# Chunks of the output weights asked for earlier and in program order, and the second half's low parts on VectorE

## The chip, the core and the metric

The kernel runs on one core of a Trainium2 chip. The metric is the device time of one launch in microseconds. A core has TensorE (PE, matmuls), VectorE (DVE), ScalarE (ACT), GpSimd (POOL) and SyncE (SP, which issues the DMAs here), each with its own queue of instructions. An engine takes its queue in order, and instructions on different engines wait for each other by semaphores.

## The reference

One layer of a hybrid block on 1024 tokens (and 16 meta tokens ahead of them) of width 1024, in f32. Cut to the part that matters:

```
z = einsum('bld,dn->bln', rmsnorm(h), w_in)      # pooled part, attention, gates ga and gb
...
o = rmsnorm(o, gla_norm) * silu(r)               # chunked gated linear attention
y_b = einsum('blc,cd->bld', o, w_gla_out)        # 512 -> 1024
m = sigmoid(ga) * y_a + sigmoid(gb) * y_b        # the merge
h = h + einsum('bld,de->ble', m, w_out)          # the out projection, 1024 -> 1024
h = h + squared_relu_mlp(rmsnorm(h, norm_ffn))
```

## The kernel before, in words

Every f32 matmul is made of three matmuls on split operands: a number is stored as a high part (rounded to the type fp32r) and a low part (what is left), and `mm3` (L246 to L248) adds high by high, high by low and low by high in PSUM. So an operand costs two steps before TensorE can use it: ACT copies it into the high part, and DVE or GpSimd subtracts that from it for the low part.

The stretch at stake lies between the end of the attention and the out projection, and runs once. It has two parts.

The blocks. `yb_block(n, h)` computes y_b and the merge for one half h of the sequence (512 tokens) and 256 of the 1024 columns, in two units. A unit is 12 matmuls into one PSUM bank, then on DVE L1093 (times the gate gb) and L1094 (plus the gated y_a, loaded from memory), then on ACT L1097, the high part `th`, and on GpSimd L1098, the low part `tl`. The gates `gl` and `ml` come from memory into `t` and `o` buffers by `yb_load` (L1041, L1042), a few units ahead. Half 0 runs while the attention's second half closes (L1299 to L1314 are the attention's last norm and its result `yg`, which half 1 needs); half 1 has four blocks, eight units, called units 1 to 8 below. Each block needs a weight of w_gla_out, split by `W1`: loaded to a raw buffer (L101), high part L77 on ACT, low part L78 on DVE or GpSimd. Half 1 uses two weights that half 0 left in place, then two new ones, whose splits follow units 2 by 2.

The out projection. `out_tile(t, ch)` makes 128 tokens by 512 columns with 24 matmuls, from `th`/`tl` of all columns and `wo`, the split of w_out. The half `ch` of w_out comes in four chunks of 256 rows: `load_wo(ch, kk)` loads a chunk to a raw buffer (L101), ACT makes the high part (L1378), DVE the low part (L1379). Matmuls 1 to 6 of a tile read chunk 0, 7 to 12 chunk 1, and so on. Then DVE adds the bank to `acc` (L1411), into which `x_again` (L1370) has loaded x.

`acc` is 32 KB of each partition and lies over what the attention used until its end, among it the buffers `t1` and `o` of half 0's units.

What sets the order. Steps are called in one order of the program, and a scheduler places the instructions of each engine by when it expects them to be ready. From `early_gates` to `wo1_open` that is switched off for ACT and DVE: their queues hold the steps in the order of the program. SP's queue is placed by the scheduler. The steps of half 1 and of the out projection are:

```
yb(0), yb(1), load_wo(0,0), yb(2), load_wo(0,1), yb(3), load_wo(0,2), load_wo(0,3), wo1_open,
x_again(0), out_tile(0,0), x_again(1), out_tile(1,0), x_again(2), out_tile(2,0), load_wo(1,0), ...
```

Of the kernel before, what the change touches and what calls it, by code (L numbers as in the profile page):

```python
# [58 lines left out]
class Ring:  # L59


    def __init__(self, nc, raw, hi, lo, depth):
        self.nc, self.raw, self.hi, self.lo, self.depth = nc, raw, hi, lo, depth
        self.queue, self.loaded, self.done, self.kept = [], 0, 0, 0
        self.views = {}
        self.eng = nc.vector

    def top_up(self):
        while self.loaded < min(self.done + self.depth, len(self.queue)):
            ap = self.queue[self.loaded]  # L70
            s = self.loaded % self.depth
            n = 1
            for k in ap.shape[1:]:
                n *= k
            raw = self.raw.load(ap, n)
            hi, lo = self.hi[:, s, :n], self.lo[:, s, :n]
            self.nc.scalar.activation(hi, raw, ACT.Copy)  # L77
# [28 lines left out]
def kernel(  # L106
# [934 lines left out]
        nc.sync.dma_start(gl, gb_dram[d, h])  # L1041
        nc.sync.dma_start(ml, ma_dram[d, h])  # L1042

    def in_order(on):


        if on:
            S["order"] = tc.manual_schedule(engines={mybir.EngineType.Activation, mybir.EngineType.DVE})
            S["order"].__enter__()
        else:  # L1050
            S.pop("order").__exit__(None, None, None)
# [14 lines left out]
    def yb_block(n, h):  # L1066
        j = YB[h][n]

        def fn(*wbs):
            if h == 0 and n > 1:  # L1070
                kept[j] = wbs[0]
            wb = wbs[0] if wbs else kept[j]
            hi, lo = (t.rearrange("p (k c) -> p k c", k=4) for t in wb)
            assert h or ("o", 0) in done
            yg = S["yg"][h]
            for e in range(2):
                d, w = 2 * j + e, slice(e * P, (e + 1) * P)
                for m in range(2 + h):
                    yb_load(2 * n + e + m, h)
                gl, ml = staged[2 * n + e, h]  # L1080
                b = bank("mm")
                for k in range(4):
                    mm3(
                        b, 1, lambda i: (hi[:, k, w], lo[:, k, w]),
                        lambda i: (yg[:, 0, k], yg[:, 1, k]), first=k == 0, last=k == 3,
                    )
                    yield 3 * 512 / 2400
                if e and not wbs:
                    W1.done, W1.kept = W1.done + 1, W1.kept - 1
# [3 lines left out]
                dve.tensor_tensor(gl, b, gl, ALU.mult)  # L1093
                dve.tensor_tensor(gl, gl, ml, ALU.add)  # L1094
                th = MH[h][:, d]
                tl = ML[h][:, d]
                act.activation(th, gl, ACT.Copy)  # L1097
                pool.tensor_tensor(tl, gl, f32(th), ALU.subtract)  # L1098

        return fn  # L1100

# [256 lines left out]
    def merge_open():  # L1358
# [4 lines left out]
        S["wo"] = [left.push("wo0", [P, 2, KT, HALF], F32R)]  # L1363
        S["left_acc"] = left.mark()
        S["acc"] = left.push("acc", [P, 8, D], F32)
        raw.lend(S["raw3"])
        nc.sync.dma_start(gB, bcast(norm_ffn))

    def x_again(t):
        nc.sync.dma_start(S["acc"][:, t], x[t * P : (t + 1) * P, :])  # L1370

    def load_wo(ch, kk):
        def fn():
            wo = S["wo"][ch][:, :, 2 * kk : 2 * kk + 2]
            c = slice(ch * HALF, (ch + 1) * HALF)
            r = raw.load(w_out[kk * 256 : (kk + 1) * 256, c].rearrange("(k p) c -> p k c", p=P), D)
            r = r.rearrange("p (k c) -> p k c", k=2)
            act.activation(wo[:, 0], r, ACT.Copy)  # L1378
            dve.tensor_tensor(wo[:, 1], r, f32(wo[:, 0]), ALU.subtract)  # L1379

        return fn

    step(one, merge_open)
    def wo1_open():
        in_order(False)
        raw.back()
        right.pop_to(0)
        buffer("u2", 2, D)
# [343 lines left out]
```

## Time and profile before

| what | value |
|---|---|
| median of 3 runs | 1234.57 us (1233.56 to 1236.65) |
| the profiled execution | 1233.45 us, span 1231.7 us |
| TensorE busy in the span | 1204.4 us, 98% |
| DVE, ACT, GpSimd busy | 851.8, 618.7 and 64.4 us |
| matmuls | 6818 |
| data moved | 173.84 MB |

The profile is of one execution. Its rows name a line of the kernel, an engine, an operation and the buffers as out<-in; "b_..." are PSUM banks. A time in brackets is the idle time of the engine just before the instruction, with what ended it. Matmuls overlap, so the row of one shows 0.39 us where one starts every 0.23 us.

### The profile page before, as it was taken

What the parts mean: (1) busy time and instruction counts of PE and PEld (TensorE: products, weight loads), DVE (VectorE), ACT (ScalarE), POOL (GpSimd) and SP (SyncE); (2) the same over time, 40 slices, a digit from 0 to 9 for tenths busy, and PEclk for the clock granted to TensorE, in tenths of its full rate; (3) what the DMA queues carried; (4) which work ended last, traced back from release to release, by engine and by line L of the source; (5) the groups of instructions that cost most, each with busy time, mean ns of one, the idle gap of its engine ahead of it and who ended that gap; (6) DMA issues with size and microseconds to landing.
All of it is one profiled execution on the core that took longest, in us unless ns stands there. A gap on an engine that the chain in (4) does not pass through costs nothing.

```text
span 1231.7 us, 18293 instructions
## 1 busy us (share of the span) xinstructions
PE 1204.4 (98%) x6818; PEld 1003.1 (81%) x6818; DVE 851.8 (69%) x1391; ACT 618.7 (50%) x1099; POOL 64.4 (5%) x70
## 2 busy tenths in 40 slices
PE   7999999999999999899999999999999999999997
PEld 7878888978887888688878888888888888888886
DVE  7986675753566676624896676776765887887686
ACT  7667567322446753312654454554554444444554
POOL 2000000001101115300000000000000000000000
PEclk9999999999999999899999999999999999999999
DMA  8043426155112156831244444444469973333532
GB/s 252 2 112 118 121 86 188 52 171 188 36 36 71 60 156 213 294 99 52 99 125 160 156 154 139 163 154 143 163 222 314 345 264 95 98 99 95 164 99 87
DMA packets 141672, 173.84 MB, mean 141 GB/s; under 512 B 9944, under 2 KB 81392, under 8 KB 141584
## 3 DMA queue, kind: packets, MB, share of 16 engines
q1 hardware_dynamic: 141552, 172.62, 43.8%
q8 instruction: 53, 0.87, 0.3%
q14 instruction: 35, 0.29, 0.1%
q0 software_dynamic: 32, 0.07, 0.1%
HBM read 119.17 MB, written 53.48 MB: 140 GB/s over the span
## 4 chain that ended last, share of the span: by engine, by line
PE 85%; DVE 9%; ACT 3%; issue 2%; DMA 1%; POOL 0%; SPq 0%; DVEq 0%; ACTq 0%; POOLq 0%
PE b_mm L246 10%; PE b_mm L247 10%; PE b_mm L248 10%; PE b_ms L247 9%; PE b_ms L246 9%; PE b_ms L248 9%; PE b_x L247 8%; PE b_x L248 8%; PE b_x L246 8%; PE b_sc L1180 1%; PE b_mx L246 1%; PE b_m L1282 1%; PE b_mx L247 1%; PE b_mx L248 1%; DVE t L1093 1%
## 5 line engine op out<-in xcount | busy, mean ns | idle before, releaser
L246 PE MATMUL b_mm<-th,w1h 128*128 128x512 f32 (+1 forms) x312 | 117.6, 377 | 1.4 <-DVE c L794 1.0
L247 PE MATMUL b_mm<-tl,w1h 128*128 128x512 f32 (+1 forms) x312 | 116.0, 372 | 0.6 <-DVE tl L1440 0.6
L248 PE MATMUL b_mm<-th,w1l 128*128 128x512 f32 (+1 forms) x312 | 115.8, 371 | 0.0
L246 PE MATMUL b_x<-th,w1h 128*128 128x512 f32 (+1 forms) x240 | 90.7, 378 | 0.0
L247 PE MATMUL b_x<-tl,w1h 128*128 128x512 f32 (+1 forms) x240 | 90.6, 378 | 0.0
L248 PE MATMUL b_x<-th,w1l 128*128 128x512 f32 (+1 forms) x240 | 90.3, 376 | 0.0
L264 ACT ACTIVATE w1h<-raw 128x512 fp32r<-128x512 f32 x96 | 59.5, 621 | 34.2 <-PE b_x L247 14.2
L265 DVE TENSOR_TENSOR w1l<-raw,w1h 128x512 fp32r<-128x512 f32 x96 | 65.6, 684 | 10.5 <-ACT w1h L264 10.5
L246 PEld LDWEIGHTS b_mm<-th,w1h 128*128 128x128 f32 x312 | 58.6, 188 | 13.1 <-issue 1.4
L264 ACT ACTIVATE w1h<-fs 128x512 fp32r<-128x512 f32 x72 | 45.4, 631 | 45.8 <-PE b_ms L247 31.3
L247 PEld LDWEIGHTS b_mm<-tl,w1h 128*128 128x128 f32 x312 | 58.6, 188 | 10.6 <-DVE tl L1440 0.9
L248 PEld LDWEIGHTS b_mm<-th,w1l 128*128 128x128 f32 x312 | 58.6, 188 | 10.3
L264 ACT ACTIVATE w1h<-bt 128x512 fp32r<-128x512 f32 x44 | 27.8, 632 | 67.9 <-issue 63.6
L265 DVE TENSOR_TENSOR w1l<-fs,w1h 128x512 fp32r<-128x512 f32 x72 | 49.3, 685 | 14.7 <-ACT w1h L264 14.6
L1589 DVE TENSOR_TENSOR bt<-w,w 128x512 f32<-128x512 f32 x80 | 54.6, 683 | 2.1 <-DMA w<-in_w_ff_dram 2.1
L248 PEld LDWEIGHTS b_x<-th,w1l 128*128 128x128 f32 x240 | 45.1, 188 | 8.4
L246 PEld LDWEIGHTS b_x<-th,w1h 128*128 128x128 f32 x240 | 45.0, 188 | 8.5
L247 PEld LDWEIGHTS b_x<-tl,w1h 128*128 128x128 f32 x240 | 45.1, 188 | 8.3
L264 ACT ACTIVATE fxh<-bt 128x512 fp32r<-128x512 f32 x36 | 22.8, 632 | 54.9 <-issue 49.3
L247 PE MATMUL b_ms<-wo,w1h 128*128 128x512 f32 x128 | 49.8, 389 | 0.0
L246 PE MATMUL b_ms<-wo,w1h 128*128 128x512 f32 x128 | 49.8, 389 | 0.0
L248 PE MATMUL b_ms<-wo,w1l 128*128 128x512 f32 x128 | 49.8, 389 | 0.0
(445 smaller groups left out, 3353.9 us busy)
## 6 DMA issues: line engine op xcount, KB each, us to landing
hf_dram<-h SPq DMA_DIRECT2D x112, 256.0 KB, 2.1
raw<-hf_dram SPq DMA_DIRECT2D x112, 256.0 KB, 2.7
w<-in_w_ff_dram SPq DMA_DIRECT2D x64, 256.0 KB, 5.0
raw<-in_w_in_dram SPq DMA_DIRECT2D x24, 512.0 KB, 4.8
raw<-in_w_ff_dram SPq DMA_DIRECT2D x16, 512.0 KB, 4.2
rawx<-in_w_ff_dram SPq DMA_DIRECT2D x16, 512.0 KB, 4.1
xs<-in_x_dram SPq DMA_DIRECT2D x8, 512.0 KB, 5.9
rawx<-in_w_in_dram SPq DMA_DIRECT2D x8, 512.0 KB, 4.3
```

The lines of the kernel that those rows point to most:

```text
L246: pe.matmul(ps, ah, bh, start=first and i == 0, stop=False, skip_group_check=more)
L247: pe.matmul(ps, ah, bl, start=False, stop=False, skip_group_check=more)
L248: pe.matmul(ps, al, bh, start=False, stop=last and i == n - 1, skip_group_check=more)
L264: act.activation(hi, a, ACT.Copy)
L265: dve.tensor_tensor(lo, a, f32(hi), ALU.subtract)
L1093: dve.tensor_tensor(gl, b, gl, ALU.mult)
L1180: pe.matmul(b[to, e, j], kk[r, s], qq[r, s], start=True, stop=True, tile_position=(e * CH, u * CH))
L1282: pe.matmul(o[part(u), e, j], scc[part(u), e, j], v[part(u), j, e], start=j == 0, stop=False, tile_position=(u * CH, u * CH), skip_group_c ...
L1589: dve.tensor_tensor(bt, w, S["w2"][q[3:]][:, i], ALU.add if q[2] == "+" else ALU.subtract)
```

## The change

Lines below `fetch` have numbers 6 to 24 higher after the change: L1093, L1094, L1097 and L1098 become L1100, L1101, L1104 and L1105, L78 becomes L84, L1378 and L1379 become L1402 and L1403, and L1411 becomes L1435. A fetch of w_out into acc or into the buffer `raw3` stands at L1394, the gain of the next norm (`gB`) at L1380, x at L1383.

- A chunk of w_out can be asked for (`fetch_wo`) apart from its split. Chunk 0 is fetched in `early_gates`, into the buffer `raw3`, which was unused until `merge_open` and is no longer lent to the raw buffers. Chunk 1 is fetched in `merge_open`, into the sixth tile of `acc`, chunk 2 behind block 0 into the seventh, and chunk 3 behind block 1 into the eighth. The two new weights of half 1 are asked for in `merge_open` too (`W1.fetch(2)`).
- The splits `load_wo(0, n)` stand ahead of block n of half 1, not behind it.
- From `merge_open` to `first_blocks` SP's queue holds its DMAs in the order of the program.
- In half 1 the low part `tl` is made on DVE.
- The load of gB stands behind the blocks, and x is asked for two tiles ahead.

```diff
+    def fetch(self, count):
+        for ap in self.queue[self.loaded + len(self.fetched) :][:count]:
             ...
+            self.fetched.append((self.raw.load(ap, n), n))
...
     def early_gates():
-        in_order(True)
+        in_order("order", mybir.EngineType.Activation, mybir.EngineType.DVE)
...
         S["raw3"] = right.push("raw3", [P, D], F32)
+        fetch_wo(0, 0, S["raw3"])
         for n in range(3):
             yb_load(n, 1)
...
                 act.activation(th, gl, ACT.Copy)
-                pool.tensor_tensor(tl, gl, f32(th), ALU.subtract)
+                (dve if h else pool).tensor_tensor(tl, gl, f32(th), ALU.subtract)
...
         S["acc"] = left.push("acc", [P, 8, D], F32)
-        raw.lend(S["raw3"])
+        any_order("order")
+        in_order("loads", mybir.EngineType.SP)
+        in_order("order", mybir.EngineType.Activation, mybir.EngineType.DVE)
+        W1.fetch(2)
+        fetch_wo(0, 1, S["acc"][:, 5])
+
+    def load_gB():
         nc.sync.dma_start(gB, bcast(norm_ffn))
...
+    def fetch_wo(ch, kk, at=None):
+        c, rows = slice(ch * HALF, (ch + 1) * HALF), w_out[kk * 256 : (kk + 1) * 256]
+        ap = rows[:, c].rearrange("(k p) c -> p k c", p=P)
+        if at is None:
+            at = raw.load(ap, D)
+        else:
+            nc.sync.dma_start(at.rearrange("p (k c) -> p k c", k=2), ap)
+        fetched[ch, kk] = at.rearrange("p (k c) -> p k c", k=2)
...
     for n, j in enumerate(YB[1]):
+        step(one, load_wo(0, n))
         if n < 2:
             step(one, yb_block(n, 1))
         else:
             step(one, yb_block(n, 1), W1, [rows4(w_gla_out, j)])
-        if n:
-            step(one, load_wo(0, n - 1))
-    step(one, load_wo(0, 3))
+        if n < 2:
+            step(one, lambda kk=n + 2: fetch_wo(0, kk, S["acc"][:, 4 + kk]))
+    step(one, load_gB)
     step(one, wo1_open)
+    step(one, lambda: x_again(0))
+    step(one, lambda: x_again(1))
     for t in range(8):
-        step(one, lambda t=t: x_again(t))
+        if t < 6:
+            step(one, lambda t=t: x_again(t + 2))
         step(one, out_tile(t, 0))
...
     def first_blocks():
+        any_order("loads")
```

TensorE's instructions stand in the same order before and after. On SP, at the attention's close, this stood before (a number behind a buffer's name is its place in memory; t_2709 and o are the gates of half 0, t_4531 and o_4535 those of half 1, mix is the attention's):

```order
L1299 DMA mix<-r_dram 128x2x512
L101 DMA raw_119<-in_w_gla_out_dram 128x4x256
L101 DMA raw_4539<-in_w_gla_out_dram 128x4x256
L1042 DMA o<-ma_dram 128x512
L1041 DMA t_2709<-gb_dram 128x512
L1042 DMA o<-ma_dram 128x512
L1041 DMA t_2709<-gb_dram 128x512
L1042 DMA o<-ma_dram 128x512
L101 DMA raw_115<-in_w_out_dram 128x2x512
L1041 DMA t_2709<-gb_dram 128x512
L1042 DMA o<-ma_dram 128x512
```

And this stands there now, on from the same load of mix:

```order
L1306 DMA mix<-r_dram 128x2x512
L107 DMA raw_119<-in_w_gla_out_dram 128x4x256
L1048 DMA o<-ma_dram 128x512
L1047 DMA t_2709<-gb_dram 128x512
L1048 DMA o<-ma_dram 128x512
L1047 DMA t_2709<-gb_dram 128x512
L107 DMA raw_115<-in_w_gla_out_dram 128x4x256
L1047 DMA t_2709<-gb_dram 128x512
L1048 DMA o<-ma_dram 128x512 x2
L1047 DMA t_2709<-gb_dram 128x512
L1394 DMA acc<-in_w_out_dram 128x2x512
L1047 DMA t_4531<-gb_dram 128x512
```

The second new weight has moved behind four gates of half 0, and chunk 0's load is gone from here (it stands well ahead). Chunk 1's fetch into acc is behind the last gate of half 0, with half 1's gates behind it. Ahead of these rows, around the load of half 0's last weight, SP had:

```order
L1041 DMA t_4531<-gb_dram 128x512 x3
L1042 DMA o_4535<-ma_dram 128x512 x3
L101 DMA raw_115<-in_w_gla_out_dram 128x4x256
L1026 DMA gb_dram<-o 128x512
L1041 DMA t_2709<-gb_dram 128x512 x2
L1042 DMA o<-ma_dram 128x512 x2
```

and now has:

```order
L1047 DMA t_4531<-gb_dram 128x512 x3
L1394 DMA raw_4539<-in_w_out_dram 128x2x512
L1048 DMA o_4535<-ma_dram 128x512 x2
L1032 DMA gb_dram<-o 128x512
L1048 DMA o_4535<-ma_dram 128x512
L1047 DMA t_2709<-gb_dram 128x512 x2
L1048 DMA o<-ma_dram 128x512 x2
L107 DMA raw_115<-in_w_gla_out_dram 128x4x256
```

The weight has moved behind four gates of half 0, and chunk 0's fetch stands among half 1's first gates. On DVE, units 1 to 4 of half 1 read like this before (th and tl are the merged result, tl not made here; raw_4539 is the second new weight):

```order
L1093 TENSOR_TENSOR t_4531<-b_mm,t_4531 128x512
L1094 TENSOR_TENSOR t_4531<-t_4531,o_4535 128x512
L78 TENSOR_TENSOR w1l<-raw_119,w1h 128x1024
L1093 TENSOR_TENSOR t_4531<-b_x,t_4531 128x512
L1094 TENSOR_TENSOR t_4531<-t_4531,o_4535 128x512
L1093 TENSOR_TENSOR t_4531<-b_x,t_4531 128x512
L1094 TENSOR_TENSOR t_4531<-t_4531,o_4535 128x512
L78 TENSOR_TENSOR w1l<-raw_4539,w1h 128x1024
L1093 TENSOR_TENSOR t_4531<-b_mm,t_4531 128x512
L1094 TENSOR_TENSOR t_4531<-t_4531,o_4535 128x512
L1379 TENSOR_TENSOR wo_4804<-raw_115,wo_4804 128x1024
```

and units 1 to 3 read like this now:

```order
L1100 TENSOR_TENSOR t_4531<-b_mm,t_4531 128x512
L1101 TENSOR_TENSOR t_4531<-t_4531,o_4535 128x512
L1105 TENSOR_TENSOR tl_143<-t_4531,th_139 128x512
L84 TENSOR_TENSOR w1l<-raw_119,w1h 128x1024
L1100 TENSOR_TENSOR t_4531<-b_x,t_4531 128x512
L1101 TENSOR_TENSOR t_4531<-t_4531,o_4535 128x512
L1105 TENSOR_TENSOR tl_143<-t_4531,th_139 128x512
L1403 TENSOR_TENSOR wo_4805<-acc,wo_4805 128x1024
L1100 TENSOR_TENSOR t_4531<-b_x,t_4531 128x512
L1101 TENSOR_TENSOR t_4531<-t_4531,o_4535 128x512
L1105 TENSOR_TENSOR tl_143<-t_4531,th_139 128x512
L84 TENSOR_TENSOR w1l<-raw_115,w1h 128x1024
```

Each unit has a third instruction, L1105, and chunk 1's split (from acc) stands behind unit 2, where the first split of a chunk stood behind unit 4. Chunks 2 and 3 follow behind units 4 and 6. Chunk 0's split has moved further up, into the attention's close, where DVE had this:

```order
L1093 TENSOR_TENSOR t_2709<-b_mm,t_2709 128x512
L1094 TENSOR_TENSOR t_2709<-t_2709,o 128x512
L1287 COPY small<-b_m_4639 128x2
L1093 TENSOR_TENSOR t_2709<-b_mm,t_2709 128x512
L1094 TENSOR_TENSOR t_2709<-t_2709,o 128x512
L1304 TENSOR_REDUCE small<-mix 128x8
```

and now has this:

```order
L1100 TENSOR_TENSOR t_2709<-b_mm,t_2709 128x512
L1101 TENSOR_TENSOR t_2709<-t_2709,o 128x512
L1294 COPY small<-b_m_4640 128x2
L1100 TENSOR_TENSOR t_2709<-b_mm,t_2709 128x512
L1403 TENSOR_TENSOR wo_4805<-raw_4539,wo_4805 128x1024
L1101 TENSOR_TENSOR t_2709<-t_2709,o 128x512
L1311 TENSOR_REDUCE small<-mix 128x8
```

The low part of chunk 0 (L1403) stands between the two instructions of one unit of half 0, ahead of the norm's sum (L1304, now L1311).

More of the change, by code (lines that the diff above doesn't have):

```diff
@@ L63, in __init__ @@
         self.nc, self.raw, self.hi, self.lo, self.depth = nc, raw, hi, lo, depth
-        self.queue, self.loaded, self.done, self.kept = [], 0, 0, 0
+        self.queue, self.loaded, self.done, self.kept, self.fetched = [], 0, 0, 0, []
         self.views = {}
         self.eng = nc.vector
[L68 to L71, printed above, removed]
+    def fetch(self, count):
+        for ap in self.queue[self.loaded + len(self.fetched) :][:count]:
             n = 1
@@ L74, in top_up @@
                 n *= k
-            raw = self.raw.load(ap, n)
+            self.fetched.append((self.raw.load(ap, n), n))
+    def top_up(self):
+        while self.loaded < min(self.done + self.depth, len(self.queue)):
+            s = self.loaded % self.depth
+            if not self.fetched:
+                self.fetch(1)
+            raw, n = self.fetched.pop(0)
             hi, lo = self.hi[:, s, :n], self.lo[:, s, :n]
@@ L1042, in yb_load, with in_order, any_order @@
         nc.sync.dma_start(ml, ma_dram[d, h])
[L1044 to L1051, printed above, removed]
+    def in_order(key, *engines):
+        S[key] = tc.manual_schedule(engines=set(engines))
+        S[key].__enter__()
+    def any_order(key):
+        S.pop(key).__exit__(None, None, None)
     def early_gates():
-        in_order(True)
+        in_order("order", mybir.EngineType.Activation, mybir.EngineType.DVE)
         left.pop_to(S["left_n"])
@@ L1370, in x_again @@
         nc.sync.dma_start(S["acc"][:, t], x[t * P : (t + 1) * P, :])
+    fetched = {}
+    def fetch_wo(ch, kk, at=None):
[6 more added lines that the diff above has]
+        fetched[ch, kk] = at.rearrange("p (k c) -> p k c", k=2)
     def load_wo(ch, kk):
         def fn():
[L1374 to L1377, printed above, removed]
+            if (ch, kk) not in fetched:
+                fetch_wo(ch, kk)
+            wo, r = S["wo"][ch][:, :, 2 * kk : 2 * kk + 2], fetched.pop((ch, kk))
             act.activation(wo[:, 0], r, ACT.Copy)
@@ L1384, in wo1_open @@
     def wo1_open():
-        in_order(False)
+        any_order("order")
         raw.back()
```

## The prediction

> **What bounds the kernel now.** I began with the page, then went through windows of 20 us to find where TensorE is not full in the stretch that the change touches, then read that place in TensorE's timeline, in the waits and in windows of 2 us.
>
> ```profile
> span 1231.7 us, 18293 instructions
> 500.00:520.00 20.00, 13.88 (x55) 10.32 (x54) 14.10 (x16) 8.24 (x11) 6.92 (x6) 0.89 0.93 320
> 520.00:540.00 20.00, 20.00 (x85) 16.41 (x84) 9.48 (x12) 5.25 (x7) 0.00 (x0) 0.94 0.63 193
> ```
>
> The columns after the length are the busy time of PE, weight loads, DVE, ACT and GpSimd, then the granted clock, the DMA share and GB/s. TensorE is busy 13.88 of 20 us and then all of it, so it is the bound on both sides of one hole: there, and only there, a microsecond saved is one at the end. TensorE's timeline (start, duration, idle before and its releaser) gives the hole's shape:
>
> ```profile
> 488.35 0.39 PE L247 MATMUL b_mm<-yg,w1h 128*128 128x512 f32 x1
> ...
> 503.53 0.39 PE L248 MATMUL b_x<-yg,w1l 128*128 128x512 f32 x1
> ...
> 505.80 0.39 PE L246 MATMUL b_mm<-yg,w1h 128*128 128x512 f32 x1
> ...
> 508.52 0.39 PE L246 MATMUL b_mm<-wo,th 128*128 128x512 f32 x1
> ...
> 511.83 0.50 PE L247 MATMUL b_mm<-wo,th 128*128 128x512 f32 x1 [1.37 <-DVE wo L1379]
> ...
> 517.31 0.79 PE L246 MATMUL b_mm<-wo,th 128*128 128x512 f32 x1 [4.06 <-ACT wo L1378]
> ...
> 518.80 0.79 PE L247 MATMUL b_mm<-wo,th 128*128 128x512 f32 x1 [0.69 <-DVE wo L1379]
> ...
> 519.82 0.63 PE L246 MATMUL b_mm<-wo,th 128*128 128x512 f32 x1
> ...
> 522.38 0.49 PE L246 MATMUL b_mm<-wo,th 128*128 128x512 f32 x1
> ...
> 523.17 0.39 PE L246 MATMUL b_x<-wo,th 128*128 128x512 f32 x1
> ...
> 534.05 0.39 PE L246 MATMUL b_mm<-wo,th 128*128 128x512 f32 x1
> ```
>
> The first two rows belong to the blocks and are used below. 505.80 is the first matmul of the last unit (12 matmuls) of the second half, 508.52 that of out tile 0 (24), 523.17 that of tile 1, 534.05 that of tile 3. A unit takes 2.72 us, one matmul 2.72 / 12 = 0.227, a tile in steady state (534.05 - 523.17) / 2 = 5.44. Tile 0 takes 14.65: **9.21 us too much**, the ceiling of what the change can return here. Idle makes 1.37 + 4.06 + 0.69 = 6.12 of it, most of the rest is a slower clock (six matmuls from 519.82 to 522.38, 0.43 each). What was waited for (us in total, times, the longest), and windows of 2 us:
>
> ```profile
> DVE wo L1379 <- ACT wo L1378: 7.1, 4, 3.0
> ACT wo L1378 <- DMA raw<-in_w_out_dram: 6.1, 2, 3.1
> PE b_mm L246 <- ACT wo L1378: 4.1, 1, 4.1
> ...
> 512.00:514.00 2.00, 1.25 (x5) 0.69 (x5) 1.17 (x3) 0.63 (x1) 0.16 (x1) 1.00 0.81 279
> 514.00:516.00 2.00, 0.00 (x0) 0.00 (x0) 1.62 (x2) 0.32 (x1) 1.10 (x1) 0.94 0.83 236
> 516.00:518.00 2.00, 0.69 (x1) 0.29 (x1) 0.71 (x1) 2.00 (x3) 1.27 (x1) 0.50 1.03 383
> ```
>
> The chain is: chunk of w_out still in flight, ACT's high part, DVE's low part, TensorE. The loads come late at 236 to 383 GB/s, and after the idle the clock stands at 0.50.
>
> **The change part by part.** TensorE's instructions keep their order. (1) The four chunks are asked for early, so the load ahead of ACT's split goes. (2) Eight low parts of the second half go from GpSimd to DVE, ahead of the chunk's split. (3) Chunk 0's split moves up into the attention's close. What is late next is DVE, whose queue now holds everything. Its prices, and those of its partners ACT and GpSimd, from their timelines and one group of the page:
>
> ```profile
> 473.90 0.69 DVE L1093 TENSOR_TENSOR t<-b_mm,t 128x512 f32<-128x512 f32 x1 [0.74 <-PE b_mm L248]
> 474.63 0.69 DVE L1094 TENSOR_TENSOR t<-t,o 128x512 f32<-128x512 f32 x1
> ...
> 485.97 1.23 DVE L1314 TENSOR_TENSOR yg<-mix,yg 128x1024 fp32r<-128x1024 f32 x1 [1.13 <-ACT yg L1313]
> ...
> 489.78 0.68 DVE L1093 TENSOR_TENSOR t<-b_mm,t 128x512 f32<-128x512 f32 x1
> 490.49 1.07 DVE L1094 TENSOR_TENSOR t<-t,o 128x512 f32<-128x512 f32 x1
> ...
> 504.17 1.47 DVE L1379 TENSOR_TENSOR wo<-raw,wo 128x1024 fp32r<-128x1024 f32 x1 [1.65 <-ACT wo L1378]
> 505.56 0.68 DVE L1093 TENSOR_TENSOR t<-b_mm,t 128x512 f32<-128x512 f32 x1
> ...
> 520.94 1.21 DVE L1379 TENSOR_TENSOR wo<-rawx,wo 128x1024 fp32r<-128x1024 f32 x1
> 473.71 1.06 ACT L77 ACTIVATE w1h<-raw 128x1024 fp32r<-128x1024 f32 x1 [0.39 <-PE b_mm L247]
> 475.35 0.63 ACT L1097 ACTIVATE th<-t 128x512 fp32r<-128x512 f32 x1 [0.58 <-DVE t L1094]
> 502.55 0.63 ACT L1097 ACTIVATE th<-t 128x512 fp32r<-128x512 f32 x1 [3.23 <-DVE t L1094]
> 503.09 1.05 ACT L1378 ACTIVATE wo<-raw 128x1024 fp32r<-128x1024 f32 x1
> 492.68 1.29 POOL L1098 TENSOR_TENSOR tl<-t,th 128x512 fp32r<-128x512 f32 x1
> L265 DVE TENSOR_TENSOR w1l<-raw,w1h 128x512 fp32r<-128x512 f32 x96 | 65.6, 684 | 10.5 <-ACT w1h L264 10.5
> ```
>
> The new operation on DVE has a direct price: L265's low part of the same size takes 0.68 (GpSimd takes 1.29). A unit on DVE, counted from the start of L1093: L1094 0.71 later (489.78 to 490.49), done after 0.69, th 0.03 behind that (474.63 + 0.69 to 475.35), so th starts at 1.43; it takes 0.63, and the low part runs from 2.09 to 2.77. The next L1093 starts at about 2.72: **2.7 a unit**, TensorE's own pace. Where a weight split stands behind the unit, ACT starts its high part 0.54 behind th (502.55 to 503.09), it takes 1.05, DVE's low part starts 0.03 later (504.14 to 504.17), at 3.05, and takes 1.21 to 1.22 with GpSimd quiet; the next L1093 starts 0.08 before its end (504.17 + 1.47 against 505.56): **4.19 a unit**, 1.47 more than TensorE needs. Splits stand behind units 1 and 3 (weights of the blocks) and 2, 4 and 6 (chunks 1, 2, 3).
>
> Start of the line. Chunk 0's low part now sits between L1093 at 473.90 and its L1094, so that L1094, th, the norm behind it and yg come about 1.16 later. From 485.97 on DVE ran without a gap, so unit 1 starts at 489.78 + 1.16 = 490.94. TensorE first reads yg's low part at 488.35 and it was done at 487.20: 1.15 of cover, so TensorE loses at most 0.1 there; without that cover it would lose the whole 1.16. Unit 1 pays 0.38 more, since GpSimd still works at the first half's last low part (L1094 took 1.07 for 0.69): 4.57.
>
> The Trainium skill (SBUF — State Buffer, "Who interferes with whom") says that a DVE instruction with two inputs in SBUF and a GpSimd instruction that reads SBUF lock each other out for a whole instruction. By that rule unit 1 would lose up to a whole GpSimd instruction, 1.29, and the sum would come out 0.9 us later; the rows bear out the contention, but only in part of its size (0.38 here).
>
> Chunk 1. Its fetch goes into acc, which lies over buffers that GpSimd's last first-half low part reads. Before, the first load into acc was let go by the same event, which SP's queue shows (its first two rows are for the rivals):
>
> ```profile
> 461.63 0.38 SPq L101 DMA_DIRECT2D raw<-in_w_gla_out_dram  x1
> ...
> 465.70 1.89 SPq L1042 DMA_DIRECT2D o<-ma_dram  x2
> ...
> 484.89 0.32 SPq L1041 DMA_DIRECT2D t<-gb_dram  x1
> 492.74 0.33 SPq L1370 DMA_DIRECT2D acc<-in_x_dram  x1
> DMA to landing us min/median/max: 3.8/6.5/8.8
> DMA to landing us min/median/max: 3.9/5.7/7.1
> ```
>
> The first landing row is of the loads into acc, the second of those into raw, both for 455 to 545. The fetch is issued at 492.74 + 1.16 = 493.9. I take the shortest landing, 3.8, since nothing was issued since 484.89 and the queues are empty; bounds 3.8 and 8.8. It lands at 497.7, and ACT could take it at 490.94 + 4.57 + 1.43 + 0.54 = 497.48: 0.2 late, so unit 2 takes 4.4. Chunk 2 stands on SP behind the gates that take unit 1's buffers, free at 490.94 + 2.8, so it leaves by 494.4 and ACT wants it behind unit 4's th, at 490.94 + 4.57 + 4.4 + 4.19 + 1.97 = 506.1; chunk 3 stands behind the gates that take unit 3's buffers (499.9 + 2.8) and leaves by 503.6, wanted at 513.0. Both have more than the longest landing, 8.8, and are costed at nothing; were that cover gone, each us would be one at the end.
>
> Sum: 490.94 + 4.57 + 4.4 + 4.19 + 4.19 + 2.72 (unit 5) + 4.27 (unit 6 to the end of chunk 3's low part, 3.05 + 1.22) = 515.28. TensorE, never held, would read that low part at matmul 19 of tile 0 and one more, 508.52 + 18 x 0.227 + 0.23 = 512.83. So TensorE is **2.45 late** in place of 9.21. Of these, 0.65 appear earlier, at the weights behind unit 3: 490.94 + 4.57 + 4.4 + 4.27 = 504.18 against the read at 503.53. With some 0.2 for restarts 2.65, and the gain is 9.21 - 2.65 = about 6.5. The out tiles need x and the norm gain behind the chunks on SP: x for tile 0 comes late for DVE, but its bank is wanted again only four tiles on, over 10 us of cover. Unit 8's low part stands behind that too and is read by tile 4, near 533.
>
> The profiled execution spans 1231.7 and lasts 1233.45; the median of the runs is 1234.57, 1.1 above. The sum gives 1226.95 for the former and **1228.1** for the latter.
>
> **The rivals.** *Chunk 1 lands late* (0.18): at acc's median of 6.5 it stands at 500.4, 2.9 late, and the gain is 6.5 - 2.7 = 3.8, 1230.8; at 8.8 it is 5.2 late, the gain 1.5, 1233.1. For it speak the 320 GB/s of that stretch before, against it the queues that are empty when the fetch leaves.
>
> *The clock drops once more* (0.08). Two short stalls remain, 0.65 and about 1.8. A stall of 1.37 kept 1.00, one of 4.06 brought 0.50. If the two trip it all the same, nine matmuls at 0.43 instead of 0.23 cost 1.8: 1229.9, still faster. The Trainium skill (TensorE: Matmul & The Clock Gate, "Part 1: The HAM clock gate (the "warmup" mystery)") says that the clock halves after an idle window of about 3.4 us; by that it would stay full here, and the trace agrees, with full clock behind 1.37 and half behind 4.06.
>
> *Slower* (0.12): SP's program order holds the load of the first half's last weight block, issued at 461.63 before, behind four more gate loads, the last two of which left at 465.70 to 467.59; it leaves at about 468. ACT's high part of it (473.71 before) stands ahead of a th (475.35 before, 476.5 with chunk 0's split) and of the norm's first step. It takes 1.06, so the point from which it decides is a landing at 475.5: each us behind that moves the norm, yg and DVE's whole line by one. The gain of 6.5 is used up at 482; at 486 it is 4.0 slower, 1238.6. Against it: raw's longest landing, 7.1, gives 475.1. For it: the load would have to wait for one more transfer ahead of it, and no row shows that queue with its loads held in program order, so more waits there are possible.
>
> That the change does not do what it says is excluded by the order of the instructions, in which SP's fetches and DVE's low parts stand where it puts them.
>
> **How the numbers follow.** 0.3%, 3.7 us, is what a measurement of this kernel can tell from no change. The forecast has 0.62; its own range runs from the ceiling (gain 9.2, 1225.4) to a chunk 1 that lands 2.7 later (1230.8). With the clock rival, faster has 0.70. The late landing lies mostly within the bound, 0.18, and slower has 0.12. The range goes from 1225.4 to 1233.1, the end of the late landing, and leaves out the slower case.
>
> **What would show it.** Right: out tile 0 takes some 8 us in place of 14.65; the longest stall in it is under 2.5 and its releaser DVE's low part of chunk 3; no wait of ACT for w_out over 1 us; the clock near 1.00; yg 1.1 to 1.2 later than before. Wrong: ACT waiting for acc's DMA for several us; ACT's high part of the gla weights waiting for DMA near 475 with TensorE idle behind it.

## The result and the profile after

The changed kernel takes 1231.51 us (median of 12 runs, 1227.94 to 1233.01) against 1234.16 for the kernel before (12 runs): a ratio of 0.9978, interval 0.9970 to 0.9985. It is faster, by 2.65 us where 6.5 were forecast. Run again later on one chip beside the kernel before, it took 1230.16 against 1234.24, ratio 0.9969 (0.9958 to 0.9980).

The profiled execution took 1232.42 us, its span is 1230.7. Windows of 20 us, with the columns as before:

```profile
480.00:500.00 20.00, 18.45 (x85) 14.78 (x84) 16.37 (x24) 6.32 (x10) 6.59 (x5) 1.00 0.36 113
500.00:520.00 20.00, 17.68 (x75) 13.46 (x74) 14.37 (x19) 7.07 (x9) 0.00 (x0) 1.00 0.64 207
520.00:540.00 20.00, 20.00 (x90) 16.59 (x89) 9.75 (x12) 4.88 (x5) 0.00 (x0) 1.00 0.90 335
```

From 500 to 520 TensorE is busy 17.68 us in place of 13.88, at full clock. But it now idles from 480 to 500 too, where it was full; this is that row of the kernel before:

```profile
480.00:500.00 20.00, 20.00 (x94) 16.65 (x93) 15.24 (x19) 7.49 (x10) 10.57 (x7) 1.00 0.45 143
```

TensorE's timeline after:

```profile
483.70 1.09 PE L1317 MATMUL b_m<-ident,mix 128*128 128x128 f32 x8 [1.53 <-DVE mix L1313]
...
505.41 0.50 PE L252 MATMUL b_x<-yg,w1h 128*128 128x512 f32 x1 [0.54 <-ACT w1h L83]
...
506.67 0.50 PE L254 MATMUL b_x<-yg,w1l 128*128 128x512 f32 x1 [0.52 <-DVE w1l L84]
...
511.80 0.39 PE L252 MATMUL b_mm<-wo,th 128*128 128x512 f32 x1
...
516.53 0.50 PE L252 MATMUL b_mm<-wo,th 128*128 128x512 f32 x1 [0.49 <-ACT wo L1402]
...
517.79 0.50 PE L253 MATMUL b_mm<-wo,th 128*128 128x512 f32 x1 [0.76 <-DVE wo L1403]
...
519.06 0.39 PE L252 MATMUL b_x<-wo,th 128*128 128x512 f32 x1
...
620.75 0.49 PE L252 MATMUL b_mm<-th,w1h 128*128 128x512 f32 x1 [0.89 <-ACT th L1463]
...
621.88 0.50 PE L253 MATMUL b_mm<-tl,w1h 128*128 128x512 f32 x1 [0.64 <-DVE tl L1464]
```

Out tile 0 runs from 511.80 to 519.06, 7.26 us in place of 14.65, and its stalls are short. It starts 3.28 later than before, though (508.52), because TensorE idled 1.53 us ahead of the norm's transposes (L1317) and 0.54 and 0.52 in the blocks, and lost some more at each restart. Tile 1 starts at 519.06 against 523.17, 4.11 earlier. The execution was already 0.44 us ahead at the start of the stretch (L1093 at 473.90 before, L1100 at 473.46 now), so the change brought 4.11 - 0.44 = **3.67 us** here. This lead at out tile 1, less what stood at the start, is the measure used below.

DVE's line, then the rows of GpSimd, ACT and SP that explain it:

```profile
473.46 0.69 DVE L1100 TENSOR_TENSOR t<-b_mm,t 128x512 f32<-128x512 f32 x1 [0.73 <-PE b_mm L254]
474.07 1.22 DVE L1403 TENSOR_TENSOR wo<-raw,wo 128x1024 fp32r<-128x1024 f32 x1
475.20 2.90 DVE L1101 TENSOR_TENSOR t<-t,o 128x512 f32<-128x512 f32 x1
479.71 1.22 DVE L1311 TENSOR_REDUCE small<-mix 128x8 f32<-128x1024 f32 x1 [1.61 <-ACT mix L1308]
...
492.36 0.68 DVE L1100 TENSOR_TENSOR t<-b_mm,t 128x512 f32<-128x512 f32 x1
...
496.94 0.68 DVE L1100 TENSOR_TENSOR t<-b_x,t 128x512 f32<-128x512 f32 x1
...
502.34 0.68 DVE L1100 TENSOR_TENSOR t<-b_x,t 128x512 f32<-128x512 f32 x1
...
506.54 0.68 DVE L1100 TENSOR_TENSOR t<-b_mm,t 128x512 f32<-128x512 f32 x1
...
513.46 0.69 DVE L1100 TENSOR_TENSOR t<-b_x,t 128x512 f32<-128x512 f32 x1
...
516.51 1.23 DVE L1403 TENSOR_TENSOR wo<-acc,wo 128x1024 fp32r<-128x1024 f32 x1 [0.25 <-ACT wo L1402]
```

```profile
474.64 2.90 POOL L84 TENSOR_TENSOR w1l<-raw,w1h 128x1024 fp32r<-128x1024 f32 x1 [1.29 <-ACT w1h L83]
500.10 1.06 ACT L1402 ACTIVATE wo<-acc 128x1024 fp32r<-128x1024 f32 x1 [1.08 <-DMA o<-ma_dram]
495.34 0.38 SPq L1394 DMA_DIRECT2D acc<-in_w_out_dram  x1
```

L1101 took 2.90 us, where the same instruction (L1094) took 0.69 before. Pushed back by chunk 0's split, it met GpSimd's low part of a block weight, which began at 474.64 and ended at 477.54. Unit 1 takes 496.94 - 492.36 = 4.58, unit 2 5.40, unit 3 4.20, units 4 and 5 together 6.92, and chunk 3's low part ends at 517.74. Unit 2 holds ACT's wait of 1.08 for chunk 1, which left SP at 495.34. (The releaser named in that row is the gate that lands beside the chunk, but ACT's instruction reads acc alone.)

One more loss lies 100 us on, where the feed-forward starts. These are a row of DVE, which waits there for a load of w_ff, and windows of 2 us:

```profile
612.08 0.69 DVE L321 TENSOR_TENSOR fs<-rawx 128x512 f32<-128x512 f32 x1 [0.81 <-DMA rawx<-in_w_ff_dram]
622.00:624.00 2.00, 2.00 (x7) 1.59 (x8) 2.00 (x4) 1.23 (x2) 0.00 (x0) 0.78 0.00 0
624.00:626.00 2.00, 2.00 (x6) 1.60 (x5) 2.00 (x4) 0.41 (x1) 0.00 (x0) 0.50 0.00 0
626.00:628.00 2.00, 2.00 (x9) 1.57 (x9) 1.27 (x4) 2.00 (x5) 0.00 (x0) 0.87 0.00 0
```

TensorE stalls there for 0.89 and 0.64 us, and the clock falls to 0.50. Before, the same two stalls were 0.42 and 0.63, and the clock stayed full:

```profile
624.35 0.50 PE L246 MATMUL b_mm<-th,w1h 128*128 128x512 f32 x1 [0.42 <-ACT th L1439]
625.48 0.50 PE L247 MATMUL b_mm<-tl,w1h 128*128 128x512 f32 x1 [0.63 <-DVE tl L1440]
```

TensorE's lead over the kernel before is 4.1 us ahead of these stalls and 2.0 at its last matmul (1221.58 against 1223.59). The span is only 1.0 shorter, because from that matmul's start to the end it took 9.07 us in this execution and 8.09 before.

### The profile page after: what moved, and what is told of

It reads as the page before. It is cut to its first block, busy times and chain, and to the rows that moved or that the text cites. A ratio compares the mean times of both kernels' runs of the same rounds, so it can differ in the third digit from the quotient of the medians.

```text
span 1230.7 us, 18292 instructions
## 1 busy us (share of the span) xinstructions
PE 1203.8 (98%) x6818; PEld 1002.2 (81%) x6818; DVE 856.4 (70%) x1399; ACT 618.4 (50%) x1099; POOL 54.1 (4%) x62
## 4 chain that ended last, share of the span: by engine, by line
PE 84%; DVE 9%; ACT 3%; issue 2%; DMA 1%; POOL 0%; SPq 0%; DVEq 0%; ACTq 0%; POOLq 0%
PE b_mm L252 10%; PE b_mm L253 10%; PE b_mm L254 10%; PE b_ms L253 9%; PE b_ms L252 9%; PE b_ms L254 9%; PE b_x L253 8%; PE b_x L252 8%; PE b_x L254 8%; PE b_sc L1187 1%; PE b_mx L252 1%; PE b_m L1289 1%; DVE t L1101 1%; PE b_mx L254 1%; PE b_mx L253 1%
```

## The experiments

My theory after the result: DVE's line from the attention's close to chunk 3's low part sets the end, as forecast, and two of its terms were too small, the split in the close (GpSimd shuts L1101 out) and chunk 1's landing. The rivals are that the low parts on DVE, or the order on SP, cost what is missing.

| kernel | median us | before, same chip | ratio, interval | lead at out tile 1, us |
|---|---|---|---|---|
| changed, again | 1230.16 | 1234.24 | 0.9969 (0.9958, 0.9980) | 3.48 |
| low parts back on GpSimd | 1230.54 | 1233.73 | 0.9970 (0.9960, 0.9979) | 6.28 |
| chunk 0's split out of the close | 1226.72 | 1233.73 | 0.9949 (0.9935, 0.9962) | 6.77 |
| GpSimd in halves | 1228.22 | 1233.73 | 0.9960 (0.9946, 0.9974) | 4.80 |
| chunk 1 early | 1228.14 | 1233.73 | 0.9956 (0.9944, 0.9969) | 4.84 |
| before + low parts on DVE | 1234.27 | 1233.72 | 1.0009 (1.0000, 1.0018) | -0.27 |
| splits inside the units | 1224.53 | 1233.72 | 0.9928 (0.9916, 0.9941) | 9.21 |
| the same, low parts on GpSimd | 1225.08 | 1233.72 | 0.9929 (0.9916, 0.9941) | 9.21 |
| changed, no order on SP | 1229.42 | 1233.72 | 0.9963 (0.9950, 0.9976) | 4.04 |
| splits inside, one load twice | 1224.14 | 1234.24 | 0.9918 (0.9902, 0.9933) | 8.34 |
| splits inside, no order on SP | 1224.70 | 1234.24 | 0.9924 (0.9911, 0.9936) | 9.21 |
| splits inside, DVE one more | 1224.97 | 1233.91 | 0.9931 (0.9918, 0.9945) | 9.08 |

**The changed kernel again**, nothing edited.

> The changed kernel once more, with nothing edited, for its spread and a second profile. Theory: its time is decided by two events beside the plan. One is whether L1101 is shut out by GpSimd (2.90 us, as in the first profile); the other is whether the feed-forward's first load that TensorE waits for lands late enough that two stalls together reach 1.5 us and the clock halves for 3.4 us (2.1 us lost). The first should recur in this profile, since the instructions stand the same; the runs should fall between 1228 (neither stall trips) and 1233. Rival (the loss of 2.1 us belongs to the change): every run at 1231 or above.

The second profile shows the same two events. L1101 takes 2.90 us again, and TensorE idles ahead of the transposes. The stalls at the feed-forward's start (0.92 and 0.63) bring half clock, and the lead over before falls from 3.94 to 1.85. The first event stands in both profiles of the changed kernel, so it belongs to the change. The second is worth 2 us and probably belongs to some of its runs only: the profiled execution spanned 1229.8 us and the five others 1227.7 to 1228.3, but those have no trace. The times fell between 1229.49 and 1231.75.

**Chunk 0's split out of the close.**

```diff
 def merge_open():
...
+    load_wo(0, 0)()
     any_order("order")
...
-    step(one, load_wo(0, n))
+    if n:
+        step(one, load_wo(0, n))
...
```

> The changed kernel with chunk 0's split taken out of the attention's close: it stands on DVE between the second and the third instruction of the second half's first unit, where DVE waits 0.70 us for th anyway. Theory (the delayed L1101 ran into GpSimd's 2.9 us low part of a block weight, so that the split cost 2.58 us and not 1.16): L1101 there takes 0.69 again, the norm and yg come 2.5 us earlier, TensorE's idle 1.53 us ahead of the norm's transposes goes, DVE's line gains 2.58 less some 0.5 that the split costs in its new place: about 2 us faster than the changed kernel, 1229.3 to 1230. Rival (DVE's line is not the bound there, or only the 1.16 of the split itself counts): 0 to 0.7 us faster.

DVE's timeline, with the split now behind unit 1's L1101:

```profile
473.62 0.69 DVE L1101 TENSOR_TENSOR t<-t,o 128x512 f32<-128x512 f32 x1
475.93 1.22 DVE L1311 TENSOR_REDUCE small<-mix 128x8 f32<-128x1024 f32 x1 [1.61 <-ACT mix L1308]
...
490.52 2.29 DVE L1404 TENSOR_TENSOR wo<-raw,wo 128x1024 fp32r<-128x1024 f32 x1
492.74 0.68 DVE L1105 TENSOR_TENSOR tl<-t,th 128x512 fp32r<-128x512 f32 x1
```

L1101 takes 0.69 again, TensorE has no idle ahead of the transposes, and the lead is 6.77, 3.1 more than in the changed kernel. That is more than the 2 expected. The split is held by GpSimd in its turn (2.29), yet it stands where DVE would have waited for th. Chunk 1's fetch leaves earlier too, at 491.76 in place of 495.34, since GpSimd's last low part of half 0 ends earlier.

**GpSimd in halves**, with the split left in the close. The flag `halves` is on from `early_gates` to `merge_open`:

```diff
...
-            self.eng.tensor_tensor(lo, raw, hi.bitcast(F32), ALU.subtract)
+            for c in (slice(0, n // 2), slice(n // 2, n)) if self.halves else (slice(0, n),):
+                self.eng.tensor_tensor(lo[:, c], raw[:, c], hi[:, c].bitcast(F32), ALU.subtract)
...
```

> The changed kernel, with GpSimd's low parts of the first half's last two block weights made in two instructions of 128x512 in place of one of 128x1024. Chunk 0's split stays in the close. If L1101 is shut out for the whole of the GpSimd instruction that began first (2.90 us in the changed kernel), it now takes at most 1.3 to 1.6 us, GpSimd's second half is held in its turn, and yg comes about 1.3 us earlier: some 1.3 us faster than the changed kernel. If the two share the port by turns, or L1101 was slow for another reason (the gate's transfer), it still takes 2.5 us or more and the time stays.

The row of DVE and that of GpSimd:

```profile
475.50 1.79 DVE L1104 TENSOR_TENSOR t<-t,o 128x512 f32<-128x512 f32 x1
474.95 3.49 POOL L86 TENSOR_TENSOR w1l<-raw,w1h 128x512 fp32r<-128x512 f32 x2 [1.28 <-ACT w1h L84]
```

DVE's instruction (L1104 in this kernel) takes 1.79 in place of 2.90, a little over the 1.3 to 1.6 expected, and GpSimd's pair takes 3.49. The lead grows by 4.80 - 3.67 = 1.13. So DVE was held until the one GpSimd instruction that had begun was over, and the second half then waited for DVE.

**Chunk 1 early.** `Tiles` picks one of two buffers by the tile's number, so that chunk 1 lies over other buffers of the attention:

```diff
...
-        S["acc"] = left.push("acc", [P, 8, D], F32)
+        S["acc"] = Tiles(left.push("acc", [P, 6, D], F32), left.push("acc2", [P, 2, D], F32))
...
-        fetch_wo(0, 1, S["acc"][:, 5])
+        fetch_wo(0, 1, S["acc"][:, 6])
...
-            step(one, lambda kk=n + 2: fetch_wo(0, kk, S["acc"][:, 4 + kk]))
+            step(one, lambda kk=n + 2: fetch_wo(0, kk, S["acc"][:, 7 if kk == 2 else 5]))
```

> The changed kernel with acc made of two buffers (tiles 0 to 5, and 6 and 7), and chunks 1, 2, 3 fetched into tiles 6, 7, 5. Tiles 6 and 7 lie over buffers that GpSimd doesn't read, so chunk 1's fetch does not wait for GpSimd's last low part of the first half. Theory: it leaves 6 to 8 us earlier, ACT's wait of 1.08 us for it goes, unit 2 takes 4.2 us in place of 5.4 and the end comes 1.2 us earlier, all else equal. Rival (the chunk is late because the queues carry the gates, not because of when it leaves): ACT still waits and the time stays.

SP's row of the fetch and ACT's of its split:

```profile
480.87 0.38 SPq L1404 DMA_DIRECT2D acc<-in_w_out_dram  x1
498.74 1.05 ACT L1412 ACTIVATE wo<-acc 128x1024 fp32r<-128x1024 f32 x1
```

The fetch leaves 14 us earlier than in the changed kernel, where 6 to 8 were expected. ACT takes the chunk without a wait, 0.54 behind th, and the lead is 4.84, 1.17 more: the expected 1.2.

**Low parts back on GpSimd**, all else as changed:

```diff
-                (dve if h else pool).tensor_tensor(tl, gl, f32(th), ALU.subtract)
+                pool.tensor_tensor(tl, gl, f32(th), ALU.subtract)
```

> The changed kernel with one part undone: the second half's low parts on GpSimd again; loads and splits stay where the change put them. My theory now: the end is set by DVE's line from the attention's close to chunk 3's low part, and the low parts on DVE trade 0.69 us and a 0.70 us wait for th per unit against GpSimd's contention. By the rows of before a unit with a split beside a busy GpSimd takes DVE 4.4 to 5.2 us, without one 1.33; six units give 5.2 + 5.4 + 4.8 + 4.4 + 1.3 + 4.8 = 25.9 against 25.4 measured in the changed kernel: within 1 us of the changed kernel, 1231 to 1233. Rival 1, the low parts on DVE bring the gain: 2 us or more slower than the changed kernel, near 1234. Rival 2, they cost part of the expected gain (eight waits of 0.70): 2 to 4 us faster than the changed kernel, 1228 to 1229.5.

The median lies within 1 us of the changed kernel, as the theory had it, but its profile is no clean comparison: ACT, DVE and GpSimd at the close read

```profile
474.96 1.06 ACT L83 ACTIVATE w1h<-raw 128x1024 fp32r<-128x1024 f32 x1 [0.96 <-DMA raw<-in_w_gla_out_dram]
475.58 0.69 DVE L1101 TENSOR_TENSOR t<-t,o 128x512 f32<-128x512 f32 x1
476.10 2.43 POOL L84 TENSOR_TENSOR w1l<-raw,w1h 128x1024 fp32r<-128x1024 f32 x1 [2.35 <-ACT w1h L83]
```

Here the block weight landed late and ACT waited 0.96 for it. So GpSimd began at 476.10, behind L1101, which took 0.69: the lead of 6.28 includes that luck, and 2.3 of it went at the feed-forward's start, with 1.07 and 0.64 of stall and half clock. The luck can be priced. From L1100 in the close to unit 1 this execution takes 16.91 us and the changed kernel 18.90, which is 1.99 of the 2.61 us between the leads. From unit 1 to the end of chunk 3's low part they take 24.77 and 25.38, and that difference lies in unit 2 (4.46 against 5.40), where chunk 1 came earlier; the other units take 20.31 and 19.98. So the engine of the low parts carries little of the gain here, and the pair with the splits inside the units, below, tests it without this luck.

**The low parts alone**, on the kernel before:

```diff
-                pool.tensor_tensor(tl, gl, f32(th), ALU.subtract)
+                (dve if h else pool).tensor_tensor(tl, gl, f32(th), ALU.subtract)
```

> The kernel before with one part of the change alone: the second half's low parts on DVE; loads and splits as before. Theory: the low part and its 0.70 us wait for th make a unit without a split take DVE 2.7 us in place of 1.33, a unit with a split stays near 4.2 to 4.4, so the pairs of a unit with and one without a split take about 6.9 us in place of 5.8 to 6.1, the splits of chunks 1 to 3 move back by 1 to 3 us and with them the loads that wait for their buffers: 1 to 3 us slower than before, 1235 to 1237. Rival (GpSimd's contention was what made the splits late, 1.47 to 1.84 us in place of 1.22): 0 to 2 us faster than before.

It is 0.1% slower, 1.0009 (1.0000 to 1.0018), at the edge of nothing; its lead is -0.27. I had expected 1 to 3 us. Out tile 0 waits as it did, for ACT's split of a chunk in flight:

```profile
518.12 0.80 PE L246 MATMUL b_mm<-wo,th 128*128 128x512 f32 x1 [4.22 <-ACT wo L1378]
```

**Splits inside the units.** This version takes chunk 1 early and sets every split between a unit's L1101 and its low part, chunk 0's too, which so leaves the close. Its second form has `pool` in place of `(dve if h else pool)` besides:

```diff
...
+                if e and wbs:
+                    yield "keep" if j in kept else "free"
+                dve.tensor_tensor(gl, b, gl, ALU.mult)
+                dve.tensor_tensor(gl, gl, ml, ALU.add)
                 if e and not wbs:
                     W1.done, W1.kept = W1.done + 1, W1.kept - 1
                     W1.top_up()
-                elif e:
-                    yield "keep" if j in kept else "free"
-                dve.tensor_tensor(gl, b, gl, ALU.mult)
-                dve.tensor_tensor(gl, gl, ml, ALU.add)
+                kk = {0: 0, 2: 1, 4: 2, 5: 3}.get(2 * n + e) if h else None
+                if kk is not None:
+                    load_wo(0, kk)()
                 th = MH[h][:, d]
...
-        step(one, load_wo(0, n))
...
```

> The changed kernel with chunk 1's early fetch (tiles 6, 7, 5 of acc in two buffers), and every split of half 1 (chunks 0 to 3 in units 1, 3, 5, 6, the two block weights in units 2 and 4) set into a unit: ACT makes its high part ahead of th, DVE its low part between L1101 and the unit's own low part, where DVE waited 0.70 us for th. Low parts stay on DVE. Theory (DVE's line of waits and work sets the end): a unit with a split takes 0.71 + 0.61 + 1.15 + 0.61 = 3.1 us in place of 4.2, chunk 3's low part ends some 16 us after unit 1's start and so ahead of TensorE's read; nothing is left of the hole in out tile 0 but restarts, TensorE is 8.5 to 9.2 us ahead of before at out tile 1; 1224.5 to 1225.5 where the later start of the feed-forward keeps full clock, 2 us more where it does not. Rival (something else holds the out tiles, x or a bank or the transfers): tile 0 still takes 7 us or more, no faster than 1227.

> The kernel with the splits set into the units and chunk 1's early fetch, but with the second half's low parts on GpSimd. Theory: a unit with a split takes DVE 0.71 + 0.61 + 1.2 to 1.84 = 2.5 to 3.2 us, so the hole closes here too and the time is that of its twin on DVE within 0.5 us: the engine of the low parts did not matter by itself. Rival (two inputs on DVE beside GpSimd's shut each other out often enough): DVE's splits late, over 1.5 us slower than its twin.

The window of the hole, and two units of DVE's line, with low parts on DVE:

```profile
500.00:520.00 20.00, 20.00 (x90) 16.57 (x89) 14.69 (x21) 5.39 (x8) 0.00 (x0) 1.00 0.90 316
500.25 0.68 DVE L1107 TENSOR_TENSOR t<-b_mm,t 128x512 f32<-128x512 f32 x1
500.96 0.69 DVE L1108 TENSOR_TENSOR t<-t,o 128x512 f32<-128x512 f32 x1
501.57 1.22 DVE L94 TENSOR_TENSOR w1l<-raw,w1h 128x1024 fp32r<-128x1024 f32 x1
502.71 0.68 DVE L1118 TENSOR_TENSOR tl<-t,th 128x512 fp32r<-128x512 f32 x1
503.31 0.69 DVE L1107 TENSOR_TENSOR t<-b_mm,t 128x512 f32<-128x512 f32 x1
```

A unit with a split takes 3.06 us and DVE waits for nothing in it. TensorE is busy 20.00 of 20 us. The lead is 9.21 us, the whole of the hole that the prediction measured, and the time is 1224.53, 9.2 us under the kernel before. With the low parts on GpSimd the lead is 9.21 too and the intervals fall together: with DVE's line out of the way the engine of the low parts makes no difference that these runs can tell.

**No order on SP**, in the changed kernel and with the splits inside the units:

```diff
-        in_order("loads", mybir.EngineType.SP)
...
-        any_order("loads")
...
```

> The changed kernel without the program order on SP: its DMAs are placed by the scheduler, which sets the norm's gain far earlier, chunks 2 and 3 together behind the fourth unit's gates, and x among the last gates. Theory (the order itself moves little, since chunk 1 waits for acc in both, and chunks 2 and 3 have cover): within 1 us of the changed kernel, 1230.5 to 1232.5. Rival (x among the gates delays the gates of units 6 to 8 or chunk 3): 2 us or more slower, near 1234.

> The kernel with the splits set into the units, low parts on DVE (1224.5), without the program order on SP. Theory (with the hole closed nothing waits for the loads, so their order is worth nothing): 1224 to 1225.2, TensorE as far ahead at out tile 1 as with the order. Rival (the order is what brings the chunks and gates in time): a stall in the blocks or in tile 0, over 1 us slower. Rival 2 (the order costs, since x and the next half of w_out are asked for late): over 0.5 us faster.

The leads are 4.04 against 3.67 and 3.48, and 9.21 against 9.21. The first time, 1229.42, lies under the 1230.5 to 1232.5 expected, but 0.7 us from the repeat on another chip. The order on SP brings or costs nothing that these runs can tell from zero.

**The feed-forward's start.** Two edits of the version with the splits inside the units:

```diff
         ff_quarters.load(1, 1)
+        ff_quarters.load(1, 1)
```

> The kernel with the splits set into the units, low parts on DVE (1224.5), with one load of the feed-forward's start issued twice: the quarter of w_ff that DVE waits for near 608 is loaded two times into the same buffer, 0.5 MB more, and all else is as it was. Theory (the landing of that load decides whether TensorE's two stalls there trip the clock): the load lands 1 to 2 us later, DVE's wait for it grows from about 0.6 us to 1.5 us or more, TensorE stalls by as much more, and the clock drops for 3.4 us in every run: 2.5 to 3.5 us slower, 1227 to 1228. Rival (the stalls come from DVE's own queue, not from the load, or the clock does not hang on them): within 0.7 us of 1224.5.

```diff
+        if t == 7:
+            dve.tensor_tensor(S["u3p"][:, 1], u[:, :HALF], u[:, HALF:], ALU.add)
```

> The kernel with the splits set into the units, low parts on DVE (1224.5), with one more instruction on DVE at the feed-forward's start: an addition of 128x512 into a buffer not yet in use, queued ahead of the subtraction that TensorE's last out tile waits for. The double load of the run before did not test the clock, since the scheduler moved the load's reader behind that subtraction. Here DVE is 0.6 us later at that place, TensorE's two stalls (0.67 and 0.64 in its parent) grow to about 1.9 us in all. Theory (about 1.5 us of stall there halves the clock for one period of 3.41 us, as in the changed kernel's two profiles and not in those with 1.05 to 1.31): 0.6 + 1.7 = about 2.2 us slower, 1226.3 to 1227. Rival (the clock's drop hangs on chance alone, not on the stall's length): 0.6 us slower, 1225, with full clock.

The first missed its aim: the scheduler set the load's reader ten instructions later on DVE, right ahead of the subtraction that TensorE waits for, and DVE did not wait at all. The reader in that kernel, and TensorE's one stall left:

```profile
613.62 0.68 DVE L331 TENSOR_TENSOR fs<-rawx 128x512 f32<-128x512 f32 x1
616.75 0.51 PE L263 MATMUL b_mm<-tl,w1h 128*128 128x512 f32 x1 [0.63 <-DVE tl L1477]
```

So the first of the two stalls comes, by this one profile, from DVE's reader of that load standing early in DVE's queue. The stall was gone when the reader stood later, and TensorE's lead grew by 0.3 us there, where its parent loses 0.3. (Its lead at tile 1 was 0.9 smaller, and the time came out equal or better.) In the second kernel the load landed early in the profiled run (DVE waited 0.21 for it), the stalls came to

```profile
615.35 0.49 PE L262 MATMUL b_mm<-th,w1h 128*128 128x512 f32 x1 [1.01 <-ACT th L1478]
616.35 0.50 PE L263 MATMUL b_mm<-tl,w1h 128*128 128x512 f32 x1 [0.51 <-DVE tl L1479]
```

and the clock stayed full: 1.52 us in all, where about 1.9 and half clock were expected. Two of its five runs took 1225.98 and 1226.85, the others 1224.32 to 1224.97. In the other profiles stalls of 1.53 (changed), 1.55 (the repeat, and GpSimd in halves) and 1.71 us (low parts back on GpSimd) came with half clock, and 0.63 to 1.42 with full clock.

The traces show why this 1.52 may have passed. Their records of the granted clock have its falls on a grid of 3.41 us. In the changed kernel it is at half for 3.41 us from 623.11, in the kernel before for 6.83, twice that, from 515.75; and the fall at the end of the changed kernel's span, at 1227.27, comes 604.16 us after the first, 177 steps. Counted back as many steps from the same fall in the last kernel (1220.16), a step ends at 616.00, inside the second stall (615.84 to 616.35): 1.17 us of idle lie in one step and 0.35 in the next. In the four profiles with half clock, 1.53 to 1.62 us of idle lie in the one step ahead of the fall; in no other profile does a step at this place hold more than 1.31. This fits a clock that is set step by step, from the idle within a step, but no run was made to test it. How much idle it takes is not shown either: near 398 in the kernel before, one stall of 1.63 us, within one step, kept full clock.

## Why the prediction was wrong in size

- The bound was right. The hole in out tile 0 was 9.21 us, and a version that closes it gains 9.2.
- The prices of DVE's units were right: 4.57 and 4.19 forecast, 4.58 and 4.20 measured, and the pair of units 4 and 5 at 6.92 against 6.91. So was the mechanism: the load ahead of ACT's split went, DVE's line became the late one, and the stalls that were left are at the places named, the weights behind unit 3 (0.54 and 0.52, 1.06 in all, against 0.65) and chunk 3. Of the signs that the prediction named, out tile 0 (7.26 us, its longest stall 0.76, released by chunk 3's low part) and its full clock came true. Two did not: yg came 3.0 us later and not 1.1 to 1.2, and ACT waited 1.08 us for chunk 1.
- **The step of the prediction that failed is the start of the line.** The split in the close was priced at 1.16 us, a DVE instruction with GpSimd quiet, and the 1.15 us of cover was to hold it. Unit 1 started at 492.36; before, less the 0.44 of head start, it would have been 489.34: 3.02 later, and TensorE idled 1.53. I wrote that GpSimd works nearby only for unit 1, and did not ask what L1101 would meet if it came 1.16 later. GpSimd's timeline of before has the answer, an instruction that began just behind L1094 (474.63) and not ahead of it:

```profile
474.85 2.72 POOL L78 TENSOR_TENSOR w1l<-raw,w1h 128x1024 fp32r<-128x1024 f32 x1 [0.16 <-ACT w1h L77]
```

  I had set aside the Trainium skill's rule (SBUF — State Buffer, "Who interferes with whom"), that the two lock each other out for a whole instruction, as borne out "only in part". That was a reading of an overlap near the end of GpSimd's instruction. In the close the trace agrees with it: 2.90 us behind one instruction of 128x1024 that had begun, 1.79 behind half of it, 0.69 without it.
- **The second term is chunk 1.** The fetch was released by the event named, which came later with the line (495.34, not 493.9), and it landed 4.6 us after issue, not in 3.8; unit 2 took 5.40, not 4.4. The rival of the late landing had the mechanism, and fetched early the chunk cost no wait.
- Together 3.02 - 1.16 = 1.86 and 1.0 make TensorE 2.9 us later than forecast: 6.5 less 2.9 is 3.6, and 3.67 was measured at out tile 1. The gain of the repeat's median lies near there (4.1), that of the first series 1 us below (2.65).
- What lowers the first series stands in no term of the sum. One part is the half clock at the feed-forward's start, 2 us in both profiles of the changed kernel. I had looked for a fall only in out tile 0, where the clock stayed full. By the rule on idle windows that the prediction cites, it would have stayed full here too; 1.53 us of idle in two pieces halved it, and the measurement decides. Of the twelve runs four have spans of 1229.9 us or more, all with a mean granted clock of 0.997, and the three with 0.999 have 1228.3 to 1228.6. Another part lies outside the span: in five of the twelve runs the time exceeds the span by 2.7 to 2.9 us, in the others by 1.7 to 1.8. Why is open.
- The slower rival did not come true, but its mechanism exists: in one profile ACT waited 0.96 us for that block weight.
- The order on SP and the engine of the low parts, by themselves, carry no gain that these runs can tell. The early fetches and the places of the splits are what is left; the later loads of gB and the earlier ones of x were not tested alone.

## What to carry to other kernels

Before an instruction is put into a gap, read what each engine beside it starts in the next 3 us, not only whether the instruction fits: a DVE instruction with two inputs in SBUF that slipped behind the start of a GpSimd one had to wait here until that one was over, 2.2 us more than it takes alone. Where one engine makes a value from another's (the high part on ACT, the low part on DVE), set other work that is ready into the wait instead of behind it: there were eight waits of 0.7 us in this stretch, and with the splits set into them and chunk 1 fetched early the whole hole closed. And read the clock at every stall that the shift reaches, not at the place of the change alone.

## What the runs showed of the hardware that was not expected

GpSimd held a DVE instruction with two SBUF inputs until its own instruction was over: 0.69 us became 2.90 and, with GpSimd's work in halves, 1.79. In the other direction, GpSimd's pair of halves took 3.49, where one instruction of that size takes 1.29 alone. At the feed-forward's start the clock stood at half for about 3.4 us (the windows of 2 us at 0.78, 0.50 and 0.87 lack 1.7 us of full clock) after 1.53 us of stalls in two pieces, where in the kernel before one stall of 1.37 us had kept full clock. The falls of the clock lie on a grid of 3.41 us, and 1.52 us of stalls that a step of the grid divided into 1.17 and 0.35 kept full clock.
